# Two more weight tiles in flight through the FFN of a hybrid decoder block on one core

## The chip, the cores and the metric

The kernel runs on one core of a Trainium2 chip. The metric is device time in microseconds (us). The core has a matrix engine (PE, with its weight loads listed as PEld), a vector engine (DVE), a scalar engine (ACT), GpSimd (POOL) and SyncE (SP). In this kernel SP and POOL do nothing but issue transfers: SP issues plain loads from HBM, POOL issues transfers that add what they bring to what already lies in the tile.

## The reference

A decoder block on 512 tokens of width 1024, in float32: retention (4 heads) and block-sparse attention (8 heads) side by side, gated and merged, then the part that matters here, the projection w_o and a SwiGLU FFN with a hidden width of 2816:

```python
mix = jax.nn.sigmoid(ga) * a + jax.nn.sigmoid(gb) * b
x = x + mix @ w_o[l]
h2 = rmsnorm(x, norm2_w[l])
f = (jax.nn.silu(h2 @ w_ffn_gate[l]) * (h2 @ w_ffn_up[l])) @ w_ffn_down[l]
x = x + f
```

## The kernel before, in words

**Arithmetic.** Each float32 matrix product is made of three passes: every operand is cut into a high part `h` (a cast to fp32r) and a low part `l` (operand minus high part), and PE does h*h, h*l and l*h (`mm3`). For a weight tile ACT makes the high part (`wh`, line 425) and DVE then the low part (`wl` for a tile of 1024 columns; for one of 512 columns both parts lie in one tile and the trace calls both `wh`). DVE instructions of every kind stand under line 227, where a helper records them.

**Winograd units.** Products are done as 2x2 block products with seven multiplications instead of eight. The weights of such a unit come as quarters B11, B21, B22 and as sums T1, T2, T3, T4 of quarters. The host lays the weights out in HBM as one list of chunks, `wall`. A sum is made in one of two ways: T1 and T3 arrive as a plain load by SP to which POOL adds a second chunk (line 352); T2 is added up by DVE in the tile of T1 (`raw<-raw,raw`); T4 is made in the tile of T2, once T2 has been cut into its parts, by one more adding transfer of POOL (line 389).

**The FFN.** The hidden width is worked through in four chunks of 6, 6, 6 and 4 tiles of 128. A chunk has three (the last: two) gate/up units, whose matmuls are 256 columns wide (`h` with `wh` and `wl`), and then one down unit with matmuls of 512 columns (`wh`, `wl` with `gu`, `gsh`, `gsl`, `g`). The order in a gate/up unit is `B11 T1 *1 T2 B21 B22 T3 / T4`, in a down unit `B11 B21 T1 T2 B22 T3 / T4`. What stands behind the slash is left over and run at the `*1` of the next unit. So behind the matmuls of a down unit PE runs B11 and T1 of the next chunk's first unit, and then the down unit's own T4. That T4 is added to PSUM banks whose contents DVE must first have added to the residual (`xr<-xr,pm`, line 227), and a down unit's T4 comes as one tile of 1024 columns and one of 512.

**Tiles and loads.** All tiles of 128x1024, weights that arrive (`raw`) as well as the cut parts (`wh`, `wl`) and most activations, share one pool of 47 buffers (`PAIRS`, line 34; the pool, line 182). A new tile takes a buffer that has come free, and whatever fills it waits for the last reader of the old contents. The order of every engine's instructions is the order of the Python code. Loads are not scheduled by time but by exchange: each time a raw tile is used up, `used` asks for the next load of a fixed list. The number of raw tiles in hand is changed by `more_raws(n)`: a positive `n` starts `n` loads more, a negative one lets that many of the next used-up tiles go without a new load.

```python
    def used(r):
...
        if not uses[r]:
            del raw[r]
            if wstate["drop"]:
                wstate["drop"] -= 1
            else:
                for f in load_w():
                    f()
...
    def more_raws(n):
...
        wstate["drop"] += max(-n, 0)
        for _ in range(n):
...
    wstate["cap"] = FAHEAD
    more_raws(FEXTRA)
```

`load_w` (line 338) puts the load on SP's queue (line 350) and, for T1 and T3, the adding transfer on POOL's queue at the same place of the program (line 352). Both queues work in order: an issue that waits holds up all that stand behind it. The issue of T4's transfer (line 389, in `was_split`) is written when T2's low part is. The call `more_raws(FEXTRA)` (line 1824) stands behind the w_o unit and ahead of the FFN's units; every load after it, to the end of the kernel, comes by exchange.

Of the kernel before, what the change touches and what calls it, by code (L numbers as in the profile page):

```python
# [40 lines left out]
EXTRA = 1  # L41
WIDE = 4
OEXTRA = 3
FEXTRA = -2
ORDER = (("rk", 0), ("rv", 0), ("gb", 0), ("rk", 1), ("rv", 1), ("rg", 1), ("gb", 1), ("ga", 0), ("a", 0), ("b", 0))
RLAG = (1, 2, 3)
SLAG = (1, 1, 1)
# [127 lines left out]
def hybrid_block(ctx: ExitStack, tc: tile.TileContext, wall, xin, xtok, n2, cin, out):  # L175
# [192 lines left out]
# [9 lines that stand above are left out]
# [1446 lines left out]
    wstate["cap"] = FAHEAD  # L1823
    more_raws(FEXTRA)
    for c in range(len(CHUNKS)):
# [84 lines left out]
```

## Time and profile before

| | |
|---|---|
| median of 3 runs | 779.3 us (778.19 to 779.51) |
| the profiled execution | 777.07 us |
| its span, first to last instruction | 774.9 us |
| granted PE clock | 1.000 |
| weight loads by SP, 512 KB and 256 KB | 157 and 21 |
| adding transfers by POOL, 512 KB and 256 KB | 77 and 9 |

The span and what lies around it (2.2 us) make the profiled time. In the answers of the trace a row of a timeline has the start, the duration, engine, line, operation, tiles written and read, the shape, the number of instructions merged in the row, and in brackets the idle time of the engine before it with what ended that. A busy PE there is not PE at its peak: matmuls overlap, so the distance from one start to the next tells its pace. The windows give for a stretch of time the busy time of each engine with its number of instructions, then the granted clock, the busy share of the 16 DMA engines, and GB/s.

### The profile page before, as it was taken

What the parts mean: (1) busy time and instruction counts of PE and PEld (TensorE: products, weight loads), DVE (VectorE), ACT (ScalarE), POOL (GpSimd) and SP (SyncE); (2) the same over time, 40 slices, a digit from 0 to 9 for tenths busy, and PEclk for the clock granted to TensorE, in tenths of its full rate; (3) what the DMA queues carried; (4) which work ended last, traced back from release to release, by engine and by line L of the source; (5) the groups of instructions that cost most, each with busy time, mean ns of one, the idle gap of its engine ahead of it and who ended that gap; (6) DMA issues with size and microseconds to landing.
All of it is one profiled execution on the core that took longest, in us unless ns stands there. A gap on an engine that the chain in (4) does not pass through costs nothing.

```text
span 774.9 us, 13031 instructions
## 1 busy us (share of the span) xinstructions
PE 765.9 (99%) x5058; PEld 691.0 (89%) x5058; DVE 637.6 (82%) x964; ACT 473.7 (61%) x784; POOL 74.8 (10%) x90
## 2 busy tenths in 40 slices
PE   8999999999999999999999999999999999999998
PEld 6888888889999998888888999989999899988996
DVE  6997788885787768897799998797987798787987
ACT  8665587877675489875355775535554355653642
POOL 0001000000101001100000000111000200111000
PEclk9999999999999999999999999999999999999999
DMA  9957543536768498969669216789656984679702
GB/s 331 356 130 181 130 83 74 135 101 156 194 172 199 115 241 237 272 169 305 173 208 267 60 55 162 173 209 293 158 150 160 276 226 128 163 188 281 179 5 108
DMA packets 42253, 139.53 MB, mean 180 GB/s; under 512 B 4688, under 2 KB 5712, under 8 KB 42192
## 3 DMA queue, kind: packets, MB, share of 16 engines
q1 hardware_dynamic: 29376, 95.45, 35.3%
q0 software_dynamic: 12384, 42.73, 31.2%
q8 instruction: 39, 0.64, 0.3%
q10 hardware_dynamic: 432, 0.52, 0.2%
q14 instruction: 22, 0.18, 0.1%
HBM read 136.60 MB, written 2.10 MB: 179 GB/s over the span
## 4 chain that ended last, share of the span: by engine, by line
PE 87%; DVE 4%; DMA 3%; issue 3%; ACT 2%; POOL 1%; SPq 0%; DVEq 0%; ACTq 0%; POOLq 0%
PE pm L227 79%; PE ps L227 8%; DMA raw<-wall 3%; DVE wl L227 1%; DVE raw L227 1%; ACT wh L425 1%; DVE xr L227 1%; DVE mx L227 0%; POOL raw L389 0%; ACT p L1078 0%; DVE wh L227 0%; DVE rot L227 0%; DVE gs L227 0%; DVE fb L227 0%; ACT L1078 0%
## 5 line engine op out<-in xcount | busy, mean ns | idle before, releaser
L227 DVE TENSOR_TENSOR wl<-raw,wh 128x1024 fp32r<-128x1024 f32 x215 | 259.0, 1220 | 46.1 <-ACT wh L425 42.0
L425 ACT CAST wh<-raw 128x1024 fp32r<-128x1024 f32 (+1 forms) x236 | 230.9, 1010 | 85.8 <-DVE raw L227 47.4
L227 PE MATMUL pm<-h,wh 128*128 128x256 f32 x1248 | 225.1, 283 | 0.0
L227 PEld LDWEIGHTS pm<-h,wh 128*128 128x128 f32 x1248 | 195.1, 192 | 0.6
L227 PE MATMUL pm<-h,wl 128*128 128x256 f32 x624 | 176.6, 283 | 0.0
L227 PEld LDWEIGHTS pm<-h,wl 128*128 128x128 f32 x624 | 119.8, 192 | 0.0
L227 PE MATMUL pm<-wh,hS 128*128 128x256 f32 (+1 forms) x448 | 104.0, 317 | 0.0
L227 PE MATMUL pm<-wh,hA 128*128 128x256 f32 (+1 forms) x400 | 101.4, 331 | 0.0
L352 POOL DMA_DIRECT2D raw<-wall x64 | 57.5, 911 | 415.7 <-DMA raw<-wall 174.2
L227 PEld LDWEIGHTS pm<-wh,hS 128*128 128x128 f32 x448 | 75.6, 190 | 5.3 <-issue 0.2
L227 PEld LDWEIGHTS pm<-wh,hA 128*128 128x128 f32 x400 | 69.1, 190 | 6.4 <-issue 0.3
L227 PE MATMUL pm<-wl,hS 128*128 128x256 f32 (+1 forms) x224 | 70.2, 313 | 0.0
L227 PE MATMUL pm<-wl,hA 128*128 128x256 f32 (+1 forms) x200 | 65.1, 326 | 0.0
L227 DVE TENSOR_TENSOR raw<-raw,raw 128x1024 f32<-128x1024 f32 (+1 forms) x42 | 49.5, 1182 | 0.4
L227 PEld LDWEIGHTS pm<-wl,hS 128*128 128x128 f32 x224 | 42.7, 191 | 2.5
L389 POOL DMA_DIRECT2D raw<-wall x22 | 19.0, 863 | 241.9 <-DVE wl L227 149.7
L227 PEld LDWEIGHTS pm<-wl,hA 128*128 128x128 f32 x200 | 38.1, 190 | 2.8
L227 PE MATMUL pm<-wh,gsh 128*128 128x512 f32 x112 | 39.9, 391 | 0.0
L227 PE MATMUL pm<-wh,mx 128*128 128x512 f32 x112 | 35.8, 394 | 0.3 <-DVE mx L227 0.3
L227 PE MATMUL pm<-wh,ret 128*128 128x512 f32 x112 | 35.4, 391 | 0.0
L227 DVE TENSOR_TENSOR xr<-xr,pm 128x512 f32<-128x512 f32 x54 | 35.3, 682 | 0.0
L227 PE MATMUL pm<-wh,gsl 128*128 128x512 f32 x88 | 34.2, 389 | 0.0
(260 smaller groups left out, 1291.0 us busy)
## 6 DMA issues: line engine op xcount, KB each, us to landing
raw<-wall SPq DMA_DIRECT2D x157, 512.0 KB, 5.7
raw<-wall POOLq DMA_DIRECT2D x77, 512.0 KB, 7.6
raw<-wall SPq DMA_DIRECT2D x21, 256.0 KB, 4.0
raw<-wall POOLq DMA_DIRECT2D x9, 256.0 KB, 6.3
xr<-xtok SPq DMA_DIRECT2D x4, 512.0 KB, 5.8
x<-xin SPq DMA_DIRECT2D x7, 256.0 KB, 5.0
out<-xr SPq DMA_DIRECT2D x7, 256.0 KB, 2.1
cs<-cin SPq DMA_DIRECT2D x1, 512.0 KB, 5.5
```

Source lines behind the costliest of these rows:

```text
L227: return f(out, *args, **kw)
L352: nc.gpsimd.dma_start(t[:, s], wall[c, :, s], accum_op=ALU.add)
L389: nc.gpsimd.dma_start(t[:, w], wall[chunk_of[u] + 3 * n + q[1], :, w], accum_op=ALU.add)
L425: A.copy(h, src)
```

## The change

One constant. The call on line 1824 was `more_raws(-2)` and becomes `more_raws(0)`, which does nothing: the first two raw tiles that are used up in the FFN are replaced by new loads, where before they were not.

```diff
-FEXTRA = -2
+FEXTRA = 0
```

No instruction is added or taken away, and PE, DVE, ACT and SP keep the order of theirs. Every load from there on stands at the place of the program at which the load two before it stood, so its buffer is another one and the wait ahead of it is for another reader. In tile names the program's running number grows with the order in which the code makes the tiles, and a load and the transfer that adds to it have the same number.

POOL's order changes at four places, since its issues of line 352 move with the loads and those of line 389 don't. The first is the first Winograd unit of the FFN; the other three are alike, at the ends of the first three down units. Below is POOL's queue at the end of the second down unit. Before, its T4 (`raw_6456` and the half tile `raw_6476`) stands ahead of the adding transfer for T1 of the next chunk's first unit (`raw_6775`):

```order
L352 DMA raw_6583<-wall 128x1024
L352 DMA raw_6614<-wall 128x512
L389 DMA raw_6456<-wall 128x1024
L389 DMA raw_6476<-wall 128x512
L352 DMA raw_6775<-wall 128x1024
L352 DMA raw_6819<-wall 128x1024
```

With the change the same T1 (now `raw_6619`) stands ahead of the down unit's T4 (now `raw_6410` and `raw_6443`):

```order
L352 DMA raw_6512<-wall 128x1024
L352 DMA raw_6554<-wall 128x512
L352 DMA raw_6619<-wall 128x1024
L389 DMA raw_6410<-wall 128x1024
L389 DMA raw_6443<-wall 128x512
L352 DMA raw_6795<-wall 128x1024
```

So T1's transfer moves from behind both T4 issues to ahead of them. On SP the place is that of the plain loads around the same T1. Before, B11 (`raw_6759`) and T1 (`raw_6775`) of the next chunk follow on `raw_6583` and `raw_6614`, and about 150 tile numbers lie between, those of the down unit's first part:

```order
L350 DMA raw_6549<-wall 128x512
L350 DMA raw_6583<-wall 128x1024
L350 DMA raw_6614<-wall 128x512
L350 DMA raw_6759<-wall 128x1024
L350 DMA raw_6775<-wall 128x1024
L350 DMA raw_6791<-wall 128x1024
```

With the change the same two loads are `raw_6589` and `raw_6619`, and the gap in the numbers lies behind them:

```order
L350 DMA raw_6512<-wall 128x1024
L350 DMA raw_6554<-wall 128x512
L350 DMA raw_6589<-wall 128x1024
L350 DMA raw_6619<-wall 128x1024
L350 DMA raw_6764<-wall 128x1024
L350 DMA raw_6780<-wall 128x1024
```

The row count and the order of SP's queue are the same; B11 and T1 of the next chunk are now written where `raw_6583` and `raw_6614` were.

## The prediction

> **What bounds the kernel now.** I read the page first, then PE's own waits, then the rows around them.
>
> ```profile
> span 774.9 us, 13031 instructions
> ...
> PE 765.9 (99%) x5058; PEld 691.0 (89%) x5058; DVE 637.6 (82%) x964; ACT 473.7 (61%) x784; POOL 74.8 (10%) x90
> ```
>
> PE is busy nearly throughout, so the change can only shorten time in which PE stands still (no matmul is taken away) or add such time. Among PE's waits, one line belongs to the FFN (line waiting, what ended the wait, us in total, times, longest):
>
> ```profile
> PE pm L227 <- DVE xr L227: 2.1, 2, 1.2
> ```
>
> Twice a matmul waits until DVE has read a PSUM bank. Here are the two places, and the like place at the end of the first down unit, in PE's timeline:
>
> ```profile
> 621.10 0.28 PE L227 MATMUL pm<-h,wl 128*128 128x256 f32 x1
> 622.27 0.47 PE L227 MATMUL pm<-wh,g 128*128 128x512 f32 x1 [0.89 <-DVE xr L227]
> 622.58 0.40 PE L227 MATMUL pm<-wl,g 128*128 128x512 f32 x1
> ...
> 711.33 0.28 PE L227 MATMUL pm<-h,wl 128*128 128x256 f32 x1
> 712.82 0.47 PE L227 MATMUL pm<-wh,g 128*128 128x512 f32 x1 [1.22 <-DVE xr L227]
> 713.13 0.40 PE L227 MATMUL pm<-wl,g 128*128 128x512 f32 x1
> ...
> 532.02 0.28 PE L227 MATMUL pm<-h,wl 128*128 128x256 f32 x1
> 532.14 0.40 PE L227 MATMUL pm<-wh,g 128*128 128x512 f32 x1
> 532.37 0.40 PE L227 MATMUL pm<-wl,g 128*128 128x512 f32 x1
> ```
>
> At 532 the switch from the next unit's T1 (`h,wl`) to the down unit's T4 (`wh,g`) costs nothing: the starts are 0.12 us apart, the next 0.23. At 622 they are 1.17 and 0.31 apart, at 712 1.49 and 0.31. So PE loses 1.17 - 0.12 = 1.05 and 0.08 at the second chunk's end, 1.37 and 0.08 at the third's.
>
> Why DVE is late there is told by DVE's and ACT's rows, and by the chain that ended last (start, length, what):
>
> ```profile
> 609.59 1.22 DVE L227 TENSOR_TENSOR wl<-raw,wh 128x1024 fp32r<-128x1024 f32 x1
> 616.23 1.22 DVE L227 TENSOR_TENSOR wl<-raw,wh 128x1024 fp32r<-128x1024 f32 x1 [5.42 <-ACT wh L425]
> ...
> 617.97 1.22 DVE L227 TENSOR_TENSOR wl<-raw,wh 128x1024 fp32r<-128x1024 f32 x1
> ...
> 621.44 1.28 DVE L227 TENSOR_TENSOR xr<-xr,pm 128x512 f32<-128x512 f32 x2
> ```
>
> ```profile
> 599.70 5.46 ACT L425 CAST wh<-raw 128x1024 fp32r<-128x1024 f32 x7 [3.78 <-DVE raw L227]
> ```
>
> ```profile
> 604.04 11.03 DMA raw<-wall
> ...
> 615.15 1.06 ACT wh L425
> ...
> 694.27 11.36 DMA raw<-wall
> ```
>
> ACT is done with seven casts at 605.16 and then waits until 615.15 for a weight. It has three casts to do: T1 of the next chunk, then T4's whole and half tile. DVE's order is T1's low part, a residual add, T4's low part at 617.97, an add, the half tile, a sum, and only then the two `xr` adds at 621.44 for which PE waits. The weight that comes last is T1, by POOL's queue:
>
> ```profile
> 587.41 1.75 POOL L352 DMA_DIRECT2D raw<-wall  x2 [7.01 <-DVE fb L227]
> 602.30 0.86 POOL L389 DMA_DIRECT2D raw<-wall  x1 [13.14 <-DVE wl L227]
> 603.50 0.86 POOL L389 DMA_DIRECT2D raw<-wall  x1 [0.34 <-DVE wh L227]
> 604.04 1.22 POOL L352 DMA_DIRECT2D raw<-wall  x1
> ```
>
> POOL stands 13.14 us at T4's issue, which waits for T2's low part; T1's issue stands third, starts at 604.04 and lands 11.03 us later. At 694.27 the picture repeats (11.36 us).
>
> **The change part by part.** First, the loads. SP's rows for the two loads of `raw_6583` and `raw_6614`, then for the next chunk's B11 and T1, and SP's longest wait between:
>
> ```profile
> 581.56 0.81 SPq L350 DMA_DIRECT2D raw<-wall  x2
> ...
> 595.26 1.77 SPq L350 DMA_DIRECT2D raw<-wall  x2
> ```
>
> ```profile
> SPq L350 <- PE pm L227: 12.8, 1, 12.8
> ```
>
> B11 and T1 move to the place of the first pair. That place lets a load go at about 582 to 584 instead of 595.26 to 597.03, some 13 us earlier. How long transfers take (KB, median us from issue to landing):
>
> ```profile
> raw<-wall SPq DMA_DIRECT2D x157, 512.0 KB, 5.7
> raw<-wall POOLq DMA_DIRECT2D x77, 512.0 KB, 7.6
> ```
>
> T1's plain half then lands at about 584 + 5.7 = 590. POOL's two issues of 587.41 are ahead of T1's issue and belong to loads that also move up two places, so POOL is free; T1's adding transfer is issued at about 590 and lands between 590 + 7.6 = 598 and 590 + 11.4 = 601. ACT needs it at 605.16. The cover is 4 us at the worst, so T1's wait goes.
>
> Second, T4, which is late next. Its issues stand behind T1's now, but T1's is done by 591 and T4's cannot go before 602.30 and 603.50 in any case, since they wait for DVE. With 7.6 to 11.4 us, T4's whole tile lands at 609.9 to 613.7. ACT casts T1 at 605.2 and T4 then, 1.06 us, to 611.0 to 614.8. DVE, free at 610.81, does T1's low part and an add by then, and T4's low part from 612.7 (ready sooner, but DVE's order) to 614.8. From there the old rows give the rest: 617.97 to the first `xr` add's end, 622.12 (half of the row at 621.44), is 4.15 us. So the bank is free at 616.9 to 619.0, and PE wants it at 621.22. Slack is 2.2 to 4.3 us: both stalls go entirely, and only a T4 landing after 613.7 + 2.2 = 615.9 brings one back.
>
> Third, the first down unit. The same wait is there on ACT:
>
> ```profile
> 526.09 2.52 ACT L425 CAST wh<-raw 128x1024 fp32r<-128x1024 f32 x3 [7.00 <-DMA raw<-wall]
> ```
>
> but PE's rows at 532 show no gap, so 7.00 us less of ACT's waiting is worth 0 there. The swap at the first Winograd unit is also worth 0: PE has no wait there in the list above. All other loads come earlier too, and nothing on PE waits for them: 0.
>
> Fourth, the buffers. Two more of the 47 hold arriving weights, so casts and other tiles get theirs from a later reader. Which waits that makes the trace of before cannot show. In the FFN the list has one such wait of a cast:
>
> ```profile
> ACT wh L425 <- PE pm L227: 10.3, 1, 10.3
> ```
>
> It is the cast behind the 11.36 us transfer of 694.27 above, so really a wait for T1, and no cast waits for a buffer now. From below the new waits cost 0; from above, PE's nearest need bounds them. The tightest feed around the new buffers is this low part, done at 602.01, and the matmul that reads it:
>
> ```profile
> 600.78 1.23 DVE L227 TENSOR_TENSOR wl<-raw,wh 128x1024 fp32r<-128x1024 f32 x1 [0.57 <-ACT wh L425]
> ```
>
> ```profile
> 603.46 0.39 PE L227 MATMUL pm<-wl,gsh 128*128 128x512 f32 x1
> ```
>
> A slip of up to 1.45 us is free there, and ACT has 3.78 us idle right before its seven casts to make up for slips earlier in the chunk. I take 0, nearest to those rows.
>
> The sum: 1.05 + 0.08 + 1.37 + 0.08 = 2.58, say 2.6 us. The profiled execution, 777.07 us with a span of 774.9, would be 774.5. It lies 2.2 under the median of the three runs, so on the median's scale I forecast 779.3 - 2.6 = 776.7 us, 0.33% less. About 0.2% (1.6 us) is what a measurement of this kernel tells from no change.
>
> I count from start to start, because starts 0.12 us apart lie under rows 0.28 us long. The gaps that the trace itself prints between such rows, 0.89 + 1.22 = 2.1, are the other end for the size: 777.2 us. The Trainium skill, "Perfetto Trace Analysis", Identifying the Most-Contended Engine, says that matmul busy time is not a good measure, because pipelined matmuls look smaller in the trace. The overlapping rows at 621 agree with it; by busy time the sum would be 2.1 and the time 777.2.
>
> **The rivals.** *The DMA engines are full anyway.* Windows before and after T4's issue, at both places (stretch, length, busy us of PE, PEld, DVE, ACT, POOL, clock, DMA share, GB/s):
>
> ```profile
> 582.00:602.00 20.00, 20.00 (x126) 18.11 (x125) 14.85 (x22) 8.39 (x14) 1.75 (x2) 1.00 0.66 175
> 602.00:616.00 14.00, 14.00 (x66) 11.66 (x65) 8.81 (x13) 4.01 (x6) 3.48 (x4) 1.00 0.99 249
> 672.00:692.00 20.00, 20.00 (x126) 18.15 (x126) 14.72 (x22) 8.39 (x14) 1.75 (x2) 1.00 0.65 170
> 692.00:706.00 14.00, 14.00 (x65) 11.63 (x64) 9.03 (x13) 3.69 (x6) 3.48 (x4) 1.00 1.01 244
> ```
>
> While T4 and T1 are on their way the engines are full (0.99 and 1.01), and loads that come earlier may fill the place that T1 leaves. If T4 then lands after 615.9, the stalls stay: 779.3 us; if at one end only, 778.1 or 777.8. For it speaks the full stretch. Against it: T1's 512 KB go into a stretch with a third of the engines' time free (0.66, 0.65), and T4 would have to take over 13.6 us where the longest row here is 11.36. The Trainium skill, "DMA: Bandwidth & Descriptors", Issuing engines are not separate DMA queues, speaks for this rival: transfers of SP and POOL run on the same 16 engines and interleave, so an earlier place in a queue adds no bandwidth. By that alone the time stays 779.3; the shares of 0.66 are the room the rule leaves. Chance 0.17.
>
> *Casts starve for buffers: slower.* The place is the down units' seven casts in a row (at 599.70 in the second). With two buffers fewer in turn they may each wait for a matmul that reads the tile before. PE loses what exceeds 1.45 us of slip, at three down units. It decides against the change by 0.2% when 3 x (slip - 1.45) passes 2.6 + 1.6, at a slip of 2.9 us; a slip of 3.5 us would give 776.7 + 6.2 = 782.9. For it: SP's loads already wait 12.8 us for PE to free a buffer, so none lies spare. Against: ACT is idle 39% of the span and 3.78 us just ahead. Chance 0.07.
>
> *The change does nothing for T1*: its load still waits for the buffer that PE frees at 595. Then POOL's swap still puts T1's transfer ahead, but T4's tiles follow in the same 13 us: between 776.7 and 779.3. The load's place in the program, two loads earlier, speaks against it. Chance 0.02.
>
> **How the numbers follow.** Forecast 0.74, rivals 0.17, 0.07 and 0.02. Of the forecast's 0.74 I give 0.06 to a measurement within 0.2%, as the three runs lie 1.1 under to 0.2 over their median. Faster 0.68; same 0.06 + 0.17 + 0.02 = 0.25; slower 0.07. The range reaches from 776.7 less the runs' 1.1 and a little, 775.4, up through 777.2 to the rival of no change, 779.4.
>
> **What would show it.** Right: PE's waits for `xr` are gone from the FFN; ACT's wait of some 10 us before the cast at 615.15 shrinks to some 4 us and is for T4; POOL issues T1's transfer near 590 and its T4 at about 602 as before. Wrong: T4 landing after 615.9 with the same PE gaps, or new waits of `wh` casts for PE with gaps in PE near 603 and at the like place of the next chunk.

## The result, and the profile after

| | before | after |
|---|---|---|
| median, 5 runs of each | 779.51 us (778.19 to 781.71) | 774.17 us (773.86 to 775.04) |
| the profiled execution | 777.07 us | 774.13 us |
| its span | 774.9 us | 772.4 us |

The ratio is 0.9929, 95% interval 0.9909 to 0.9948: faster, by 5.3 us where 2.6 was forecast. The two profiled executions, though, differ by 2.5 us in their spans, which is the sum of the prediction. So the first question is why the medians lie further apart than the profiles.

The page of the changed kernel:

```profile
span 772.4 us, 13041 instructions
...
PE 766.1 (99%) x5058; PEld 691.0 (89%) x5058; DVE 638.2 (83%) x964; ACT 475.1 (62%) x784; POOL 74.9 (10%) x90
```

PE does the same 5058 matmuls in the same busy time; only time in which it stood still is gone. (The count of all instructions differs by 10; they are waits on semaphores.) Its longest waits now (line, what ended the wait, us in total, times, longest):

```profile
PE ps L556 <- DVE warm L227: 1.2, 1, 1.2
PE ps L227 <- ACT p L1078: 0.4, 1, 0.4
PE pm L227 <- DVE mx L227: 0.3, 1, 0.3
```

No line for `xr` is left, and none of these lies in the FFN. At the end of the second down unit PE goes from the next unit's T1 to the down unit's T4 without a gap, the starts 0.12 and 0.23 us apart:

```profile
621.16 0.28 PE L227 MATMUL pm<-h,wl 128*128 128x256 f32 x1
621.28 0.40 PE L227 MATMUL pm<-wh,g 128*128 128x512 f32 x1
621.51 0.40 PE L227 MATMUL pm<-wl,g 128*128 128x512 f32 x1
```

POOL's queue and ACT's casts there show why. T1's adding transfer, then T4's two:

```profile
591.97 0.86 POOL L352 DMA_DIRECT2D raw<-wall  x1 [8.24 <-DMA raw<-wall]
602.36 0.86 POOL L389 DMA_DIRECT2D raw<-wall  x1 [9.53 <-DVE wl L227]
603.56 0.86 POOL L389 DMA_DIRECT2D raw<-wall  x1 [0.33 <-DMA raw<-wall]
```

T1 goes 12 us earlier than before (604.04), and T4 goes when it always went. ACT, after its seven casts (the first row), casts T1, T4 and T4's half tile:

```profile
599.75 5.46 ACT L425 CAST wh<-raw 128x1024 fp32r<-128x1024 f32 x7 [3.77 <-DVE raw L227]
605.98 1.06 ACT L425 CAST wh<-raw 128x1024 fp32r<-128x1024 f32 x1 [0.76 <-PE pm L227]
610.12 1.06 ACT L425 CAST wh<-raw 128x1024 fp32r<-128x1024 f32 x1 [3.09 <-DMA raw<-wall]
```

Before, ACT stood 9.99 us and cast T1 at 615.15. Now it waits 0.76 us for a tile and 3.09 us for T4. DVE's two `xr` adds follow at 615.99 instead of 621.44:

```profile
615.99 1.27 DVE L227 TENSOR_TENSOR xr<-xr,pm 128x512 f32<-128x512 f32 x2
```

The first add ends at about 616.6, and PE asks for the bank at 621.28: 4.6 us of cover. The windows of the changed kernel (length, busy us of PE, PEld, DVE, ACT, POOL, clock, DMA share, GB/s):

```profile
582.00:602.00 20.00, 20.00 (x126) 18.10 (x125) 14.99 (x23) 9.05 (x14) 1.94 (x3) 1.00 0.72 183
602.00:616.00 14.00, 14.00 (x66) 11.66 (x64) 14.00 (x20) 5.95 (x8) 2.83 (x4) 1.00 0.96 249
```

The share rises from 0.66 to 0.72 ahead of T4's issue, where T1's transfer now runs. Behind it the engines stay as full as they were (0.99 before, 0.96 now, 249 GB/s both times): what T1 left free, other loads fill, which also come earlier.

### The profile page after: what moved, and what is told of

The parts are those of the page before. It is cut to its first block, busy times and chain, and to the rows that moved or that the text cites. A ratio compares the mean times of both kernels' runs of the same rounds, so it can differ in the third digit from the quotient of the medians.

```text
span 772.4 us, 13041 instructions
## 1 busy us (share of the span) xinstructions
PE 766.1 (99%) x5058; PEld 691.0 (89%) x5058; DVE 638.2 (83%) x964; ACT 475.1 (62%) x784; POOL 74.9 (10%) x90
## 4 chain that ended last, share of the span: by engine, by line
PE 96%; DVE 2%; ACT 1%; DMA 1%; issue 0%; SPq 0%; DVEq 0%; ACTq 0%
PE pm L227 87%; PE ps L227 8%; DMA raw<-wall 1%; DVE mx L227 0%; ACT p L1078 0%; DVE rot L227 0%; DVE wl L227 0%; ACT L1078 0%; DVE raw L227 0%; ACT wh L425 0%; DVE p L227 0%; DVE nb L227 0%; ACT pt L1115 0%; ACT rot L1196 0%; ACT rot L1195 0%
```

## The experiments

**Where the other 2.8 us are: the kernel before once more, and three parts of the change.** No edit for the first. The second, swap_only, moves no load and alters POOL's order alone:

```diff
-            nc.gpsimd.dma_start(t[:, w], wall[chunk_of[u] + 3 * n + q[1], :, w], accum_op=ALU.add)
+            t4_held.append(lambda: nc.gpsimd.dma_start(t[:, w], wall[chunk_of[u] + 3 * n + q[1], :, w], accum_op=ALU.add))
+            if u < ffn or plan[u][0] != "X" or u == len(plan) - 1:
+                t4_held.pop()()
...
                 nc.gpsimd.dma_start(t[:, s], wall[c, :, s], accum_op=ALU.add)
+                while t4_held:
+                    t4_held.pop(0)()
```

The third, early_only, moves the loads as the change does but keeps the T1 adding transfers of the units right behind a down unit (`heads`) behind its T4, as before:

```diff
-FEXTRA = -2
+FEXTRA = 0
...
-                nc.gpsimd.dma_start(t[:, s], wall[c, :, s], accum_op=ALU.add)
+                add = lambda c=c: nc.gpsimd.dma_start(t[:, s], wall[c, :, s], accum_op=ALU.add)
+                if u in heads and q == ("T1", 0):
+                    t1_held.append(add)
+                else:
+                    add()
...
             nc.gpsimd.dma_start(t[:, w], wall[chunk_of[u] + 3 * n + q[1], :, w], accum_op=ALU.add)
+            while q[1] == 1 and t1_held:
+                t1_held.pop(0)()
```

The fourth, fextra_m1, is the change by half:

```diff
-FEXTRA = -2
+FEXTRA = -1
```

> The kernel before, once more, for the span of each of its runs and a second profile. The change took 5.3 us from the median of the timed runs but only 2.5 us from the span of the profiled execution. Theory 1 (the stalls vary): the two waits of PE at the ends of the second and third down unit depend on when T1's transfer lands, and the first profile caught a short case; the spans of the timed runs then lie 2 to 5 us above 774.9, near 777, and a second profile shows PE's waits for the residual adds adding up to more than the 2.1 us printed in the first. Theory 2 (outside the span): the spans are 775 again, and what lies around them is 4 to 5 us instead of 2. Theory 3 (another part of the kernel): spans near 777, with the waits for the residual adds at 2.1 us and the rest in stretches ahead of the FFN. The ratio to the kernel before is 1.000 for all.

Measured: 778.05 us (12 runs, 776.87 to 782.47; ratio to the other runs of the same kernel 0.9986, 0.9968 to 1.0005). Theory 1, in the main, though half of the 12 spans lie under 776, lower than it said: the profiled execution, span 777.3, has stalls that the first profile did not have. PE's waits, those of the FFN:

```profile
PE pm L227 <- DVE xr L227: 2.3, 2, 1.3
...
PE pm L227 <- DVE wl L227: 0.4, 1, 0.4
PE pm L227 <- ACT pm L1718: 0.2, 1, 0.2
```

The two new lines are the first down unit's end. PE's rows there:

```profile
529.63 0.40 PE L227 MATMUL pm<-h,wh 128*128 128x256 f32 x2
530.45 0.39 PE L227 MATMUL pm<-h,wl 128*128 128x256 f32 x1 [0.42 <-DVE wl L227]
...
536.62 0.84 PE L227 MATMUL pm<-wh,g 128*128 128x512 f32 x3
537.69 0.39 PE L227 MATMUL pm<-h,wh 128*128 128x256 f32 x1 [0.23 <-ACT pm L1718]
```

Laid over the changed kernel's profile, matmul by matmul (both have 5058, in the same order), this execution falls 1.17 us behind there, 0.28 near 555, 1.51 at the second down unit's end and 1.23 at the third's. That is 1.6 us more in the FFN than the first profile lost. Of the 2.4 us between the two spans the rest lies elsewhere: 0.35 ahead of the FFN and 0.4 behind the last matmul.

> The kernel before with POOL's order alone changed: T4's two adding transfers of the first three down units (and that of the first Winograd unit of the FFN) are issued behind T1's instead of ahead of it; no load moves. If T1's third place on POOL's queue is what costs (theory 1), T1's transfer goes at about 601, when its plain half has landed, and lands by 612; T4 lands by 615, ahead of the 615.9 at which a stall begins: the gain of the change is here almost whole, 774 to 775.5 us. If the earlier loads are what counts (rival), nothing is gained: 778.5 to 780.

Measured: 774.95 us (774.59 to 775.25), ratio 0.9937 (0.9914 to 0.996) to a before of 778.49 on the same chip. POOL's queue there, T1 first and the two T4 behind it:

```profile
602.28 0.86 POOL L352 DMA_DIRECT2D raw<-wall  x1 [14.14 <-DMA raw<-wall]
603.14 0.89 POOL L393 DMA_DIRECT2D raw<-wall  x1
604.34 0.86 POOL L393 DMA_DIRECT2D raw<-wall  x1 [0.31 <-DVE wh L227]
```

T1 is issued at 602.28 where the first profile of before has 604.04, but ahead of T4's 768 KB. ACT casts T1, then T4's whole tile, at:

```profile
611.40 1.05 ACT L431 CAST wh<-raw 128x1024 fp32r<-128x1024 f32 x1 [5.39 <-DMA raw<-wall]
615.25 1.05 ACT L431 CAST wh<-raw 128x1024 fp32r<-128x1024 f32 x1 [2.79 <-DMA raw<-wall]
```

Before, T1's cast came first too, but at 615.15, and T4's behind it. PE now has no wait in the FFN. POOL's order alone, with no tile more in flight, gives 3.5 us, as much as the change gives when it is repeated (3.4, below).

> The change with POOL's order put back: all loads two places earlier, but T1's adding transfer of the next chunk's first unit is issued behind T4's as before. If T1's place on POOL's queue is what costs (theory 1), the stall stays: T1 goes at 604 and lands at 612 to 615, 777 to 780 us. If the earlier loads are what counts (rival), 774 to 775.5 us.

Measured: 780.98 us (779.05 to 784.96), ratio 1.0025 (1.0006 to 1.0044): the earlier loads alone make it a little slower. PE's waits:

```profile
PE pm L227 <- DVE xr L227: 3.4, 2, 1.8
...
PE pm L227 <- DVE wl L227: 0.8, 1, 0.8
PE pm L227 <- ACT wh L433: 0.6, 1, 0.6
```

All three places are worse than in base_again. The DMA issues of the 12 us around T4's and T1's issue (KB, median us from issue to landing), first early_only's, then base_again's:

```profile
raw<-wall SPq DMA_DIRECT2D x4, 512.0 KB, 10.2
raw<-wall POOLq DMA_DIRECT2D x3, 512.0 KB, 11.7
```

```profile
raw<-wall SPq DMA_DIRECT2D x4, 512.0 KB, 8.5
raw<-wall POOLq DMA_DIRECT2D x3, 512.0 KB, 9.0
```

SP's four loads take longer than in any of the four profiles of before (8.3 to 8.5 us). POOL's median of three says little: in those four it lies anywhere from 8.9 to 11.4, and T4's whole tile takes 7.6 us here and 7.8 in base_again. What did grow is T1's time: from its issue to its cast 11.84 to 12.22 us at the three places, where before has 11.50 at most (the table below). The Trainium skill, "DMA: Bandwidth & Descriptors", Issuing engines are not separate DMA queues, says that DMAs interleave on the same 16 engines whichever engine starts them; that T1 takes longer when SP's loads come earlier and T1 keeps its place agrees with it. That these loads are the cause is argued from the runs, not shown by itself.

> Half of the change: one tile more in flight instead of two (the constant at -1). T1 is the second of the two loads of the next chunk, so one place earlier on SP it goes where B11 went, at 595 instead of 597, and its adding transfer is still issued behind T4's by the exchange order. Theory 1: nothing is gained, 778 to 780 us, with PE's two waits as before. If every load's earlier place counts in proportion (rival): half the gain, 776.5 to 777.5 us.

Measured: 779.65 us (776.59 to 784.85), ratio 1.0006 (0.9985 to 1.0028). T1 still stands behind T4, and nothing is gained:

```profile
PE pm L227 <- DVE xr L227: 1.0, 2, 0.7
```

So the gain is no matter of so much per tile; it comes with the step that puts T1 ahead in the queue.

**The three places apart.** The changed kernel again, then swap_only's edit at some of the down units:

```diff
-            if u < ffn or plan[u][0] != "X" or u == len(plan) - 1:
+            if u not in held_at:
```

with `held_at` the first down unit alone (swap_first), or the second and third (swap_later); and fextra_p1 with `FEXTRA = 1`. The kernel before took 778.37 us (776.25 to 780.41, 19 runs) beside them.

> The changed kernel once more, beside three others on one chip. If its time is steady because no stall in the FFN is left that hangs on when a transfer lands, its executions lie within 1.2 us of each other (774 to 775.2) while those of the kernel before spread over 4 us or more; if the spread is the chip's and not the kernel's, both spread alike.

Measured: 774.98 us (774.1 to 776.16), ratio 0.9959 (0.9946 to 0.9973). A gain of 3.4 us here, not 5.3. The executions lie 2.1 us apart, more than I had expected, before's 4.2.

> POOL's order is changed at the first down unit alone, everything else stands as before. Theory: the first down unit also costs time in most executions, and the prediction's 0 for it held only for the one it was read from; then this alone is worth 0.5 to 1.5 us of the median and its profile shows no gap of PE at 529 to 538, and gaps of 1 to 2 us each at 622 and 713 as before. Rival: that unit is worth 0, and this kernel takes the time of the one before (within 0.3 us).

Measured: 777.69 us (776.25 to 780.97), ratio 0.9994 (0.998 to 1.0007). By the medians 0.7 us, which the interval does not tell from 0. The profile has the stalls of the other two places, and at the first place none:

```profile
PE pm L227 <- DVE xr L227: 1.6, 2, 1.0
```

> POOL's order is changed at the second and third down unit alone. Theory: worth 2.6 us or more (the two stalls as read, larger in most executions), with 0.5 to 1.5 us less than the change at all three down units gave (3.5 us), and a spread that is smaller than before's but larger than that of the change at all three. Rival: the first unit is worth nothing, and this kernel reaches the changed one's time (within 0.3 us).

Measured: 776.07 us (774.64 to 777.82), ratio 0.9965 (0.9952 to 0.9979), 2.3 us. Its profiled execution has no wait for `xr`, and 1.04 us lost at the first down unit. The first place's own wait:

```profile
PE pm L227 <- DVE wl L227: 0.3, 1, 0.3
```

2.3 and 0.7 make 3.0 of the 3.4. The theory had the later two at 2.6 or more; they are a little less.

> One more step in the direction of the change: a third tile holds arriving weights from w_o on. Theory: no wait of PE in the FFN is left to take away, so the time is the changed kernel's (within 0.5 us). Rival: every tile more in flight is worth about 2 us (then 772), or the casts begin to starve for tiles (slower than the changed kernel by over 1 us, with waits of casts for PE behind it).

Measured: 774.85 us (774.19 to 776.89), ratio 0.9961 (0.9946 to 0.9976), the changed kernel's time. PE has no wait in the FFN to take away, and the casts do not starve for tiles with a third one gone either. The profiled execution is the slowest of its six (776.89), and all that it loses against the changed kernel's profile, 2.4 us, lies ahead of the FFN: 2.0 of it in the first 11 us, where the granted clock (the third number from the end) was 0.50 for a while:

```profile
7.60:10.80 3.20, 3.20 (x9) 2.55 (x8) 2.82 (x7) 3.20 (x9) 0.00 (x0) 0.50 1.06 399
```

So executions also differ in a part of the kernel that the change does not touch.

**Microsecond for microsecond.** To compare executions, I put their times on one scale: a time less what PE had by then fallen behind the changed kernel's profile, matmul by matmul. What PE lost at a place is how much further it falls behind there. T1's issue comes at the same point of PE's schedule in all executions in which T1 stands last (at 516.79, 604.10 and 693.18 us on this scale, each within 0.03), because T4's issues ahead of it wait for DVE, which works to PE's beat. So what differs is T1's time from POOL's issue to the start of its cast. In each cell that time, then what PE lost there, both in us (blank where T1 stands ahead of T4):

| execution | first | second | third |
|---|---|---|---|
| before (first profile) | 9.35, 0 | 11.11, 1.15 | 11.43, 1.47 |
| base_again | 10.99, 1.17 | 11.50, 1.51 | 11.23, 1.23 |
| fextra_m1 | 9.43, 0 | 10.59, 0.61 | 10.90, 0.93 |
| swap_first | | 11.26, 1.27 | 10.80, 0.82 |
| swap_later | 10.86, 1.04 | | |
| early_only | 12.22, 2.38 | 11.84, 1.86 | 12.04, 2.03 |

Time less loss is 9.82 to 9.84 us at the first place wherever PE lost anything, 9.96 to 9.99 at the second, 9.96 to 10.01 at the third. So PE loses what T1 takes beyond that, or, on the common scale, how far its cast starts past 516.79 + 9.82 = 526.61, past 614.07 and past 703.15. Two kernels and two more profiles of before test this:

```diff
-            if u < ffn or plan[u][0] != "X" or u == len(plan) - 1:
+            if u < ffn or plan[u][0] != "X" or u == len(plan) - 1 or q[1] == 0:
```

This is swap_mid: swap_only with T4's whole tile ahead of T1 again and only its half tile behind. In t1_late, with the loads as before, T1 is held back behind one transfer more. It has early_only's lines, but lets T1 go at another place (with the `+`):

```diff
                 if u in heads and q == ("T1", 0):
                     t1_held.append(add)
                 else:
                     add()
+                    while t1_held:
+                        t1_held.pop(0)()
```

The kernel before took 779.3 us (776.85 to 781.27, 11 runs) beside these.

> No load moved; at the three down units T1's adding transfer is issued between T4's whole and T4's half tile. Theory: PE stands still by just as much as T1's cast starts past a fixed point of PE's schedule (526.6, 614.07 and 703.15 us on the changed kernel's scale, read from five profiles in which T1 stood last). With the 256 KB half tile no longer ahead of it T1's cast starts 1 to 1.5 us earlier, so that each stall shrinks to 0 to 0.5 us: 775 to 776.5 us. Rival: what matters is T4's whole tile ahead of T1, and the time stays within 0.5 us of the one before; or T4's half tile, now last, is late in T1's place (a gap of PE with T1's cast in time).

Measured: 775.74 us (774.44 to 776.57), ratio 0.9952 (0.9934 to 0.997). POOL's queue at the second place, T1 in the middle, and PE's rows at its end:

```profile
602.24 0.86 POOL L393 DMA_DIRECT2D raw<-wall  x1 [14.88 <-DVE wl L227]
602.78 1.22 POOL L352 DMA_DIRECT2D raw<-wall  x1
603.44 1.45 POOL L393 DMA_DIRECT2D raw<-wall  x1
```

```profile
621.04 0.28 PE L227 MATMUL pm<-h,wl 128*128 128x256 f32 x1
621.66 0.47 PE L227 MATMUL pm<-wh,g 128*128 128x512 f32 x1 [0.34 <-DVE xr L227]
```

T1's cast starts at 614.66 and 703.53 on the common scale. That is 0.35 to 1.08 us earlier than in the four profiles of before, less than the 1 to 1.5 expected. The points give 614.66 - 614.07 = 0.59 and 703.53 - 703.15 = 0.38; PE lost 0.55 and 0.35, and 0 at the first place.

> No load moved; at the three down units T1's adding transfer is issued one transfer later still, behind the next unit's next adding transfer, which itself waits for its load. T1's issue comes some 6 us later. Theory (microsecond for microsecond): PE loses the whole lateness past the same three points, 5 to 8 us more at each, so 793 to 802 us, and each gap is T1's cast start less that point to within some 0.3 us. Rival: part of the lateness is taken up by work that PE or DVE does meanwhile, and the gaps are smaller than the lateness by over 1 us.

Measured: 795.75 us (793.32 to 797.85, 4 runs), ratio 1.0199 (1.0168 to 1.0231). PE loses most of it at one row, at the second place:

```profile
627.19 0.28 PE L227 MATMUL pm<-h,wl 128*128 128x256 f32 x1
631.68 0.80 PE L227 MATMUL pm<-h,wh 128*128 128x256 f32 x2 [4.22 <-ACT wh L433]
632.94 0.58 PE L227 MATMUL pm<-h,wl 128*128 128x256 f32 x1 [0.46 <-DVE wl L227]
```

The points give 7.61 and 6.87 us at the second and third place, and PE lost 7.59 and 6.83. At the first they give 5.79, and PE lost 7.75. There PE itself was slow: behind the stall the granted clock was 0.50 from 534.6 to 541.5 us, and PE went through 10 matmuls of 256 columns in 2 us, where at full clock it goes through 42 in 5 us (the second row):

```profile
536.00:538.00 2.00, 2.00 (x10) 2.00 (x11) 2.00 (x3) 0.06 (x1) 0.69 (x1) 0.50 0.91 186
545.00:550.00 5.00, 5.00 (x42) 4.96 (x41) 5.00 (x7) 3.92 (x5) 0.88 (x1) 1.00 0.54 202
```

Over its next 24 matmuls this put PE another 2.5 us behind, with no wait among them, so it came to T4 later than T4's bank was free. At the other two places the clock was 0.50 as well, but PE still met a wait at T4, and T1's lateness set the loss.

> The kernel before, one more profile. Theory: three more pairs of T1's time from issue to cast and PE's gap, on the same line: no gap below 9.8 us, above it the excess. Rival: gaps that don't follow T1's time.

Measured: 777.11 us in its one execution, span 774.9. Time and loss at the three places: 9.57 and 0, 11.44 and 1.46, 11.28 and 1.31. The first pair, T1's issue (it is the first of the two instructions in its row) and its cast:

```profile
516.58 2.11 POOL L352 DMA_DIRECT2D raw<-wall  x2
```

```profile
526.15 2.52 ACT L425 CAST wh<-raw 128x1024 fp32r<-128x1024 f32 x3 [7.23 <-DMA raw<-wall]
```

> The kernel before, a further profile, for the same pairs: T1's time from issue to cast between 9 and 12 us in all, and the first down unit's on either side of 9.8 us, so that it costs 0 in some executions and about 1 us in others. Rival: the first unit stays under 9.8 us in these and in the profile that the prediction was read from, and base_again was the odd one.

Measured: 780.75 us in its one execution, span 778.9. Time and loss: 11.34 and 1.53, 10.92 and 0.95, 11.31 and 1.32. The same pair as above, and PE's wait that follows:

```profile
517.44 1.22 POOL L352 DMA_DIRECT2D raw<-wall  x1
```

```profile
528.78 1.99 ACT L425 CAST wh<-raw 128x1024 fp32r<-128x1024 f32 x2 [9.01 <-DMA raw<-wall]
```

```profile
531.14 0.39 PE L227 MATMUL pm<-h,wl 128*128 128x256 f32 x1 [0.76 <-DVE wl L227]
```

All six pairs of the two profiles fit, within 0.05 us. The two executions run the same program; T1 takes 9.57 us in one and 11.34 in the other, and the second pays for it.

## Why the prediction was right in its mechanism and wrong in its size

*What bounds the kernel, and which row is late: right.* PE's busy time did not change. swap_only shows that moving T1 ahead of T4 in POOL's queue is enough for the gain, and early_only that the earlier loads are not.

*Loads and T1: right.* T1's transfer was issued at 591.97 (forecast: near 590), T4's at 602.36 (602.30), and T1 is no longer waited for. That the other loads come earlier was costed at 0; early_only shows that they have a price of their own, 2.5 us by the medians (0.5 to 3.4 by the interval), where T1 stays behind, and it is the swap that keeps it from counting.

*T4, late next: right.* It was cast at 610.12 (forecast: landing 609.9 to 613.7), and the bank was free at 616.6, just ahead of the 616.9 to 619.0.

*The two stalls: right for the execution that was read.* Laid matmul by matmul over the changed kernel's profile, that execution lost 1.15 + 1.47 = 2.62 us in the FFN where the sum had 2.58, and the spans differ by 2.5. Counting from start to start was right; the printed gaps (2.1) were too small. The Trainium skill, "Perfetto Trace Analysis", Identifying the Most-Contended Engine, says that matmul busy time is not a good measure of how close a kernel is to its peak, and here the printed matmul times were no good measure of a stall either. The page's reason, that pipelined matmuls look smaller in the trace, is not what these rows show, though the prediction took them to agree: rows of 0.28 us with starts 0.12 apart look larger than their pace, and so hide part of a gap.

*The first down unit, "worth 0 there": this step failed.* It took "PE's rows at 532 show no gap" for a property of the kernel. It was one of that execution: T1 took 9.35 us there, 0.47 under the 9.82 at which PE begins to lose. In base_again, base_p2 and swap_later it took 10.86 to 11.34, and PE lost 1.04 to 1.53. The rows to doubt it by stood in the first profile: ACT waited 7.00 us for that transfer, and the like transfers took 11.11 and 11.43 us at the other two places. Had the first one taken as long, PE would have lost 1.3 to 1.6 us there.

*Carrying the 2.2 us over to the median: this failed with it.* The prediction subtracted one execution's 2.6 us from the median of other executions, as if what set these 2.2 us above the profiled one would stay. It did not stay: the changed kernel's profiled execution (774.13) lies at its median (774.17). Before's profiled execution was one of its fastest, with one of three stalls missing. The four profiles of before lost 2.62, 3.91, 2.77 and 3.80 us at the three places, and two of them 0.28 and 0.27 more near 555: 3.4 us on average. That is the 778.37 - 774.98 = 3.4 measured beside after_again, but four profiles are few, and the interval there is wide (2.1 to 4.2). That the first place's stall is there in two of these four, and makes up most of what lies between 2.6 and 3.4, is shown. The way from there to the 5.3 of the first comparison is not: its interval (4.1 to 7.1 us) and that of after_again barely touch, and over all runs, 65 of before (median 778.66) and 11 of after (774.75), the difference is 3.9. Executions also differ where the change has no part: whichever the kernel, PE enters the FFN from 0.2 us ahead of the changed kernel's profile (base_p1) to 2.4 behind it (fextra_p1), and base_p2 has 1.8 us more behind its last matmul than the first profile, where its last output takes 3.9 us to land instead of 2.1. So five runs of a kernel that spreads from 776.3 to 783.2 may simply have fallen high; no profile of those five tells, and the cause of this part stays open.

*The rivals.* Full DMA engines: the engines stayed full behind T4's issue, as this rival had it, but T4 would have had to land after 615.9 and was cast at 610.12. Casts that starve: one wait of 0.76 us for a tile, at T1's cast, and PE never felt it; nor did it with a third tile gone. That the change does nothing for T1: no.

## What to carry to other kernels

A stall that one profile shows as zero, right where an engine upstream waits 7 us for a transfer, may be a margin and not a zero: look for the same transfer at like places of the same trace, and cost the stall with their times. When a profiled execution lies well under the median, ask what the others pay that it does not, before that difference is carried over unchanged. And where an in-order queue holds an issue that must wait and behind it one that need not, try changing the order alone before spending buffers on it: here it gave 774.95 us, and two tiles more 774.17 and 774.98.

## What the runs showed of the hardware that was not expected

The same adding transfer of 512 KB, issued at the same point of the schedule, took 9.35 to 11.34 us until its cast in four executions of one program, short in two (9.35 and 9.57) and long in two (10.99 and 11.34); what decides that stays open. And the loss follows that time very closely: over 22 stalls of 0.35 to 7.6 us, in ten profiles, T1's cast less PE's loss stays within 0.05 us of a fixed point at each of the three places, with one exception (t1_late's first place), where the clock came in.

Where PE stood 3.5 to 4.2 us at a stretch (t1_late), its granted clock was 0.50 for 3.4 to 6.8 us in or behind the stall, and at the first place that cost time of its own. In early_only, whose printed gaps reach 1.8 us, it stayed at 1.00 through the FFN.
